# Where attention masks are added to scores: TensorE or VectorE

## The chip, the cores and the metric

The kernel runs on one core of a Trainium2 chip. A core has a matrix engine (TensorE, PE in the profile), which writes its products to PSUM, a memory of eight banks beside the main on-chip memory (SBUF), and engines that work element by element: VectorE (DVE), ScalarE (ACT) and GpSimd (POOL). SyncE (SP) starts the transfers from device memory (DMA). Each engine takes its instructions in order; between engines semaphores say when data are ready. The metric is the time of one execution on the device in microseconds.

## The reference

Two layers of a trunk on 256 tokens of 1024 channels, in fp32. Each layer has a feed-forward part (ffn1), a mixer of four branches, cross-attention to a memory, and a second feed-forward part (ffn2). Two branches of the mixer are attentions, and these are what the change touches:

```python
y_c = nsa_attention(q_n, k_n[:, :, 0], v_n[:, :, 0], k_n[:, :, 1], v_n[:, :, 1],
                    k_n[:, :, 2], v_n[:, :, 2], g_nsa, ...)
...
y_d = banded_attention(q_s, k_s, kv_s[:, :, 1], SWA_WINDOW, swa_sinks[l]).reshape(B, S, BRANCH_W)
gates = jax.nn.sigmoid(u_gate.reshape(B, S, N_BRANCH, D))
branches = (y_a, y_b, y_c, y_d)
merged = gates[:, :, 0] * (y_a @ w_branch[l, 0])
for n in range(1, N_BRANCH):
    merged = merged + gates[:, :, n] * (branches[n] @ w_branch[l, n])
```

and in banded_attention the mask is put on the scores ahead of the softmax:

```python
mask = (diff >= 0) & (diff < window) & (kpos[None, :] >= 0)
s = jnp.einsum('bqgrd,bkgd->bgrqk', qi, ki).astype(jnp.float32) * scale
s = jnp.where(mask, s, NEG_INF)
```

The first attention (NSA, eight heads) has three parts: one over compressed blocks, one over selected blocks, which with 256 tokens are all of them, and one over a window longer than the sequence. The last two need the causal mask alone. The second attention (SWA, eight heads) sees the last 128 tokens.

## The kernel before

Each fp32 weight and each activation is split on the chip into a high part (fp32r, a copy by ScalarE, line 257) and a low part (the difference, by VectorE, line 260), and each product is three matmuls: high by high, high by low, low by high (mm3, lines 273 to 276). The helper matmul on line 271 records nearly all products, so the profile's rows are told apart by their tiles. Weights come in chunks of 2 MB as two halves, raw; ScalarE makes hi and VectorE lo from each.

In the mixer (lines 763 to 920) the tokens lie in two tiles of 128. NSA (nsa) goes through eight units: token tile t, key group g, pair of heads. score makes the scores of a unit in a PSUM bank (acc), and softmax works on them: VectorE's maximum (line 698), ScalarE's exponentials, VectorE's reciprocal. A bank is 128 x 512: for t = 0 it holds two heads by two branches by 128 keys, for t = 1 one head by two branches by 256 keys, so such a unit has two banks. value takes the probabilities (pp) of the unit before: pt_split transposes four blocks of 128 x 128 on PE into a PSUM bank tr (line 722), ScalarE makes pth and VectorE ptl of it, and pv multiplies these with the values (vp). In SWA (swa) one unit is 4 heads for t = 0 and 2 heads for t = 1.

The masks: setup copies two 128 x 128 tiles, "swal" (the window's far edge) and "tri" (causal), 0 or -1e30, to an fp32r tile msk. In score a matmul with the identity idr as the stationary side and the mask as the moving one, repeated over heads by a broadcast view (mtri4, mtri2, mswa), begins the accumulation in the bank, and the products of q with the keys (kkh and kkl in NSA, kks in SWA) are added to it. The profile writes such a product acc<-msk,idr. Per layer there are four of 512 columns and eight of 256 in NSA, and six of 512 in SWA.

Beside the attention VectorE has the taps of a depthwise convolution (conv_taps, 124 per layer, tile cy), whose sums PE takes with a matmul of ones (acc<-cy,ones), the low parts of the weights, and the merge of the branches. PE has products that depend on no attention: the gates (gate_chunk, tiles mm<-hTh,hi and so on), the branches (branch_chunk, mm<-y,hi) and the next projection (tok_major of qs: acc<-hi,hTh). They stand between the attention's steps and fill PE while the other engines work.

The order of all this isn't written out. The tile framework takes the program as written, with priorities for some steps (front, urgent), simulates it with times of its own, and fixes the order of the instructions on each engine by that, with semaphores where data or buffers need them. PSUM is three pools: mm with two buffers, acc with four, tr with two.

Of the kernel before, what the change touches and what calls it, by code (L numbers as in the profile page):

```python
# [8 lines left out]
F32R = mybir.dt.float32r  # L9
# [3 lines left out]
ALU = mybir.AluOpType  # L13
AX = mybir.AxisListType

P = 128
# [11 lines left out]
# ---------------------------------------------------------------- layouts  # L28
# [13 lines left out]
for _n, _w in (("ident", 128), ("tri", 128), ("swal", 128), ("cm", 32), ("vm", 2), ("edge", 64), ("inv", 32), ("ii", 32)):  # L42
    _COFF[_n] = (_NC, _NC + _w)
    _NC += _w
# [159 lines left out]
# ---------------------------------------------------------------- kernel  # L204


class Trunk:
# [28 lines left out]
    # ---- small helpers  # L236
# [55 lines left out]
    # ---- weight stream  # L292
# [24 lines left out]
    def use_spare(self, fn, ahead, at=None):  # L317
        """fn() makes the tiles of the chunk at this distance from the next one to be asked for; it is fetched no
        later than when the chunk at distance at is asked for."""
        self.spare[self.cur + ahead] = fn  # L320
        if at is not None:
            self.early.setdefault(self.cur + at, []).append(self.cur + ahead)
# [26 lines left out]
    # ---- set-up  # L349
# [20 lines left out]
    def setup(self):  # L370
# [12 lines left out]
        msk = self.const.tile([P, 2, P], F32R, name="msk")  # L383
        nc.vector.tensor_copy(msk[:, 0, :], c("swal"))
        nc.vector.tensor_copy(msk[:, 1, :], c("tri"))
# [74 lines left out]
    # ---- norms  # L460
# [9 lines left out]
    def mean_rstd(self, halves, f=1.0):  # L470
        """(f * (mean of squares + eps)) ** -0.5 over two halves of a row."""
# [25 lines left out]
    def boundary(self, gpost, half, gpre, hold=True):  # L497
        """What adds norm(acc) * gpost to a token tile of x, and makes the next norm's transposed halves."""
# [24 lines left out]
    def behind_turn(self, calls, n):  # L523
        """The last n of these calls' matmuls are queued behind the transposes that are pending."""
# [9 lines left out]
    # ---- products  # L534

    def ws(self, out, w, cols, src, nk, k0=0, start=True):
        """out[cols, tok] over nk K-tiles; weights stationary."""
# [4 lines left out]
    def xs_rows(self, nm, nchunks, src, by_tok=2, order=None, by_col=False, then=None):  # L542
        """[tok, 1024] = src^T @ W for chunks of two K-tiles; the last by_tok chunks go token tile by token tile,
        for the second of these in the order given; or column half by column half.  then(t, acc) takes the sums."""
# [40 lines left out]
    # ---- feed-forward  # L585
# [53 lines left out]
    # ---- mixer  # L639
# [10 lines left out]
    def tok_part(self, acc, w, h, n, k0, t, tail=None):  # L650
        """acc[tok, n] += h^T @ W for the K-tiles of one chunk."""
# [36 lines left out]
    def put_v(self, kind, t, ps):  # L688
        """ps: [tok, 2, 64]"""
# [3 lines left out]
    def softmax(self, bank, ng, w, wgt=None, nsink=None, on_dve=False):  # L693
        """bank [P, ng, w] -> normalised (and gated) [P, ng, w] on SBUF."""
# [37 lines left out]
    def pipeline(units):  # L732
        """Each unit is (scores, values): the next unit's scores go before this one's values."""
# [24 lines left out]
    def ypair(self):  # L758
        """hi and lo of four K-tiles."""
# [252 lines left out]
    def blocks(self, ctT, mp):  # L1012
        """Windows of 32 tokens plus their positions, as split [P, 8, hi | lo] tiles."""
# [19 lines left out]
    def compress(self, i, blk, hid):  # L1033
        """Half a product of the compression's first layer; hid gets it, with its bias, after the second half."""
# [51 lines left out]
    def nsa(self, qn, kkh, kkl, gt, y, before_cmp):  # L1086
# [4 lines left out]
        def score(t, g, pr):  # L1091
            h0 = g * 4 + pr * 2
            if t == 0:
                bank = self.pacc((P, 2, 2, P))
                self.matmul(bank.rearrange("p a b k -> p (a b) k"), self.idr, self.mtri4, True, False)
                for j in range(2):
                    q = qn[0][:, h0 + j, :]
                    self.matmul(bank[:, j], q, kkh[:, g, :, 0:P], False, False)
                    self.matmul(bank[:, j], q, kkl[:, g, :, 0:P], False, True)
                wt = self.s(4)  # L1100
# [4 lines left out]
            for j in range(2):  # L1105
                bank = self.pacc((P, 2, S))
                q = qn[1][:, h0 + j, :]
                self.matmul(bank[:, :, P:], self.idr, self.mtri2, True, False)
                self.matmul(bank, q, kkh[:, g], False, False)
                self.matmul(bank, q, kkl[:, g], False, True)  # L1110
                ps.append(self.softmax(bank, 2, S, gt[1][:, h0 + j, 1:3]))
# [65 lines left out]
    def swa(self, qs, kks, y, mp):  # L1177
# [4 lines left out]
        def score(t, g, pr):  # L1182
            if t == 0:
                bank = self.pacc((P, 4, P))
                self.matmul(bank, self.idr, self.mtri4, True, False)
# [168 lines left out]
```

## Time and profile before

| | us |
|---|---|
| median of three runs (1606.2 to 1607.36) | 1607.15 |
| the profiled execution, from first to last instruction | 1605.6 |
| TensorE busy (products) | 1583.0 |
| TensorE busy (weight loads, beside the products) | 1486.1 |
| VectorE busy | 1148.9 |
| ScalarE busy | 860.4 |

The engines work beside each other, so the busy times don't add up to the span. Products on PE are pipelined: one starts before the one ahead of it ends, so a row's duration is longer than the time it takes from PE, and the distance from start to start is the better price. The same holds, less strongly, on VectorE.

### The profile page before, as it was taken

How to read it: one execution, taken by the hardware profiler on the slowest of the kernel's cores; microseconds unless marked ns; L12 is line 12 of the kernel's file. 1: busy time of each engine (PE TensorE's matmuls, PEld its weight loads, DVE VectorE, ACT ScalarE, POOL GpSimd, SP SyncE). 2: the span in 40 equal slices, each digit the busy share in tenths (PEclk: the TensorE clock that was granted, in tenths of full speed). 3: DMA queues.
4: the chain of work that ended last, by engine and by line, in shares of the span. 5: the costliest groups of instructions: out<-in, count | busy, mean ns of one | idle time of the engine just before them, and what ended most of it. 6: DMA issues, size and time to landing. Idle time of an engine off the chain costs nothing.

```text
span 1605.6 us, 28410 instructions
## 1 busy us (share of the span) xinstructions
PE 1583.0 (99%) x11324; PEld 1486.1 (93%) x11324; DVE 1148.9 (72%) x1872; ACT 860.4 (54%) x1461; POOL 21.6 (1%) x44
## 2 busy tenths in 40 slices
PE   7999999999999999999999999999999999999998
PEld 6999889999998989999899988999999999899986
DVE  6665579999878566666566656799998775666653
ACT  6444455665656454444444445656665654554442
POOL 0000000000000000000000000000000000000000
PEclk9999999999999999999999999999999999999999
DMA  7555646643455654555655566465435565455552
GB/s 259 178 181 175 228 154 203 210 132 132 161 170 193 196 176 147 184 184 173 222 172 183 182 198 208 147 222 173 144 120 169 175 211 169 157 169 181 183 195 102
DMA packets 79909, 285.57 MB, mean 178 GB/s; under 512 B 8992, under 2 KB 9760, under 8 KB 79776
## 3 DMA queue, kind: packets, MB, share of 16 engines
q1 hardware_dynamic: 79776, 283.75, 53.5%
q8 instruction: 89, 1.46, 0.3%
q14 instruction: 44, 0.36, 0.1%
HBM read 282.67 MB, written 1.05 MB: 177 GB/s over the span
## 4 chain that ended last, share of the span: by engine, by line
PE 92%; DMA 2%; DVE 2%; ACT 2%; issue 1%; SPq 0%; DVEq 0%; POOLq 0%; ACTq 0%
PE mm L271 54%; PE acc L271 35%; DMA raw<-in_stream_dram 2%; PE tr L465 1%; PE tr L722 1%; ACT hi L257 1%; DVE lo L260 1%; DMA x<-in_x_dram 1%; DVE cy L268 0%; PE tr L271 0%; ACT yw L257 0%; PE tr L684 0%; DVE yw L260 0%; ACT pp L257 0%; PE tr L623 0%
## 5 line engine op out<-in xcount | busy, mean ns | idle before, releaser
L260 DVE TENSOR_TENSOR lo<-raw,hi 128x1024 fp32r<-128x1024 f32 (+1 forms) x468 | 565.8, 1215 | 270.3 <-ACT hi L257 267.4
L257 ACT ACTIVATE hi<-raw 128x1024 fp32r<-128x1024 f32 (+1 forms) x468 | 489.5, 1053 | 359.9 <-PE mm L271 231.4
L271 PE MATMUL mm<-hTh,lo 128*128 128x256 f32 x2048 | 581.6, 284 | 0.0
L271 PE MATMUL mm<-hTh,hi 128*128 128x256 f32 x2048 | 580.9, 284 | 0.4 <-ACT hi L257 0.4
L271 PE MATMUL mm<-hTl,hi 128*128 128x256 f32 x2048 | 580.0, 283 | 0.0
L271 PEld LDWEIGHTS mm<-hTh,hi 128*128 128x128 f32 x2048 | 392.4, 192 | 1.0 <-ACT hi L257 0.8
L271 PEld LDWEIGHTS mm<-hTh,lo 128*128 128x128 f32 x2048 | 392.3, 192 | 0.6
L271 PEld LDWEIGHTS mm<-hTl,hi 128*128 128x128 f32 x2048 | 392.4, 192 | 0.3
L271 PE MATMUL acc<-hi,mid 128*128 128x512 f32 x512 | 159.2, 394 | 0.0
L271 PEld LDWEIGHTS acc<-hi,mid 128*128 128x128 f32 x512 | 96.1, 188 | 23.3
L268 DVE SCALAR_TENSOR_TENSOR cy<-t,sp,cy 128x256 f32<-128x256 f32 x240 | 107.8, 480 | 0.0
L257 ACT ACTIVATE mid<-t 128x256 fp32r<-128x256 f32 x76 | 31.8, 419 | 137.5 <-DVE t L268 137.5
L271 PE MATMUL acc<-lo,mid 128*128 128x512 f32 x256 | 99.7, 397 | 0.0
L271 PE MATMUL mm<-y,hi 128*128 128x256 f32 x512 | 93.7, 282 | 0.0
L271 PE MATMUL acc<-hi,hTh 128*128 128x256 f32 (+2 forms) x272 | 87.8, 324 | 1.7 <-ACT hTh L257 1.6
L271 PE MATMUL acc<-hi,hTl 128*128 128x256 f32 (+2 forms) x272 | 87.8, 323 | 1.3 <-DVE hTl L260 1.3
L271 PE MATMUL acc<-lo,hTh 128*128 128x256 f32 (+2 forms) x272 | 87.6, 322 | 0.0
L271 PEld LDWEIGHTS mm<-y,hi 128*128 128x128 f32 x512 | 79.4, 188 | 1.0
L271 PE MATMUL mm<-y,lo 128*128 128x256 f32 x256 | 72.5, 283 | 0.0
L268 DVE SCALAR_TENSOR_TENSOR t<-t,mm 128x256 f32<-128x256 f32 x160 | 66.8, 418 | 2.6
L257 ACT ACTIVATE t<-acc 128x512 bf16<-128x512 f32 (+3 forms) x56 | 27.2, 487 | 60.4 <-PE acc L271 57.3
L260 DVE TENSOR_TENSOR mid<-t,mid 128x256 fp32r<-128x256 f32 x76 | 32.3, 426 | 36.8 <-ACT mid L257 36.8
(247 smaller groups left out, 2263.1 us busy)
## 6 DMA issues: line engine op xcount, KB each, us to landing
raw<-in_stream_dram SPq DMA_DIRECT2D x508, 512.0 KB, 4.5
g<-in_gains_dram SPq DMA_DIRECT2D x18, 512.0 KB, 4.6
raw<-in_stream_dram SPq DMA_DIRECT2D x8, 280.0 KB, 3.1
t<-in_mem_dram SPq DMA_DIRECT2D x4, 512.0 KB, 4.0
out_dram<-x SPq DMA_DIRECT2D x4, 256.0 KB, 2.0
x<-in_x_dram SPq DMA_DIRECT2D x2, 256.0 KB, 3.1
x<-in_x_dram SPq DMA_DIRECT2D x1, 512.0 KB, 9.0
t<-in_small_dram SPq DMA_DIRECT2D x2, 256.0 KB, 5.6
```

The lines of the kernel that those rows point to most:

```text
L257: return self.nc.scalar.activation(out, in_, func, **kw)
L260: return self.nc.vector.tensor_tensor(out, a, b, op=op)
L268: return self.nc.vector.scalar_tensor_tensor(out, a, s, b, op0=op0, op1=op1)
L271: return self.nc.tensor.matmul(out, lhsT, rhs, start=start, stop=stop, skip_group_check=True)
L465: tr = self.nc.tensor.transpose(pt[:, j, :], xn[:, j * P:(j + 1) * P], self.ident)
L722: self.nc.tensor.transpose(pt[:, j, :], s_, self.ident)
```

## The change

The mask product goes away. The first product of q with a key tile starts the accumulation instead (the start flag), and when the scores are complete, VectorE adds the mask to the bank in place: it reads the bank in PSUM and the mask in SBUF and writes the bank. The softmax then works on the bank as before. 36 matmuls go, 36 additions come: 20 of 128 x 512 and 16 of 128 x 2 x 128, in a bank whose second half of keys alone needs the mask. The two copies into msk go too; the masks are used as fp32 where they were loaded, and for this "swal" and "tri" change places in the table of constants. Comments are left out of the new file, so its later lines have other numbers (722 is 721, 698 is 697, 465 is 464).

```diff
-for _n, _w in (("ident", 128), ("tri", 128), ("swal", 128), ("cm", 32), ("vm", 2), ("edge", 64), ("inv", 32), ("ii", 32)):
+for _n, _w in (("ident", 128), ("swal", 128), ("tri", 128), ("cm", 32), ("vm", 2), ("edge", 64), ("inv", 32), ("ii", 32)):
...
-        msk = self.const.tile([P, 2, P], F32R, name="msk")
-        nc.vector.tensor_copy(msk[:, 0, :], c("swal"))
-        nc.vector.tensor_copy(msk[:, 1, :], c("tri"))
+        a = _COFF["swal"][0] - P
+        msk = cst[:, a:a + 2 * P].rearrange("p (a b) -> p a b", a=2)
...
             if t == 0:
                 bank = self.pacc((P, 2, 2, P))
-                self.matmul(bank.rearrange("p a b k -> p (a b) k"), self.idr, self.mtri4, True, False)
                 for j in range(2):
                     q = qn[0][:, h0 + j, :]
-                    self.matmul(bank[:, j], q, kkh[:, g, :, 0:P], False, False)
+                    self.matmul(bank[:, j], q, kkh[:, g, :, 0:P], j == 0, False)
                     self.matmul(bank[:, j], q, kkl[:, g, :, 0:P], False, True)
+                flat = bank.rearrange("p a b k -> p (a b) k")
+                self.tt(flat, flat, self.mtri4, ALU.add)
                 wt = self.s(4)
                 nc.vector.tensor_copy(wt.rearrange("p (a b) -> p a b", a=2), gt[0][:, h0:h0 + 2, 1:3])
                 p = self.softmax(bank.rearrange("p a b k -> p (a b) k"), 4, P, wt)
...
             for j in range(2):
                 bank = self.pacc((P, 2, S))
                 q = qn[1][:, h0 + j, :]
-                self.matmul(bank[:, :, P:], self.idr, self.mtri2, True, False)
-                self.matmul(bank, q, kkh[:, g], False, False)
+                self.matmul(bank, q, kkh[:, g], True, False)
                 self.matmul(bank, q, kkl[:, g], False, True)
+                self.tt(bank[:, :, P:], bank[:, :, P:], self.mtri2, ALU.add)
                 ps.append(self.softmax(bank, 2, S, gt[1][:, h0 + j, 1:3]))
             return ps
 
...
         def score(t, g, pr):
             if t == 0:
                 bank = self.pacc((P, 4, P))
-                self.matmul(bank, self.idr, self.mtri4, True, False)
                 for r in range(4):
                     q = qs[0][:, g * 4 + r, :]
-                    self.matmul(bank[:, r, :], q, kks[:, g, 0:P], False, False)
+                    self.matmul(bank[:, r, :], q, kks[:, g, 0:P], r == 0, False)
                     self.matmul(bank[:, r, :], q, kks[:, 2 + g, 0:P], False, True)
+                self.tt(bank, bank, self.mtri4, ALU.add)
                 return self.softmax(bank, 4, P, None, ns[:, g * 4:g * 4 + 4], True)
             h0 = g * 4 + pr * 2
             bank = self.pacc((P, 2, S))
-            self.matmul(bank.rearrange("p a (b k) -> p a b k", b=2), self.idr, self.mswa, True, False)
             for j in range(2):
                 q = qs[1][:, h0 + j, :]
-                self.matmul(bank[:, j, :], q, kks[:, g, :], False, False)
+                self.matmul(bank[:, j, :], q, kks[:, g, :], j == 0, False)
                 self.matmul(bank[:, j, :], q, kks[:, 2 + g, :], False, True)
+            quads = bank.rearrange("p a (b k) -> p a b k", b=2)
+            self.tt(quads, quads, self.mswa, ALU.add)
             return self.softmax(bank, 2, S, None, ns[:, h0:h0 + 2], True)
```

The framework's simulation gives other orders on PE, VectorE and ScalarE within the two mixers; the orders of SyncE and GpSimd are the same. Names carry the number of a buffer; a number in the new order is the old one less 3 for the same tile.

PE at the end of NSA in the first layer, from the transposes of probabilities (tr_3704, later tr_3701) on. acc_4608 (later acc_4605) is the next projection, acc_3359 and acc_3569 are NSA's outputs (later 3356 and 3566). Before, from the last of those transposes on:

```order
L722 MATMUL tr_3704<-ident_99,pp_3619 128x128
L271 MATMUL acc_4563<-cy_3803,ones_183 128x256
L271 MATMUL acc_4608<-lo_4611,hTh_2126 128x512
L271 MATMUL acc_4608<-hi_4610,hTl_2127 128x512
L271 MATMUL acc_4608<-hi_4610,hTh_2126 128x512
L271 MATMUL acc_4608<-lo_4611,hTh_2126 128x512
L271 MATMUL acc_4608<-hi_4610,hTl_2127 128x512
L271 MATMUL acc_4608<-hi_4616,hTh_2126 128x512
L271 MATMUL acc_4608<-lo_4617,hTh_2126 128x512
L271 MATMUL acc_4608<-hi_4616,hTl_2127 128x512
L271 MATMUL acc_4608<-hi_4616,hTh_2126 128x512
L271 MATMUL acc_4608<-lo_4617,hTh_2126 128x512
```

The rows that follow it before, up to the first use of ptl_3710, are one more product of the projection (acc_4608<-hi_4616,hTl_2127), four products of pth_3665, pth_3709 and ptl_3666, and four transposes. Now:

```order
L271 MATMUL acc_4605<-hi_4613,hTl_2124 128x512
L271 MATMUL acc_4560<-cy_3800,ones_180 128x256
L271 MATMUL acc_3356<-pth_3662,vc0_196 128x512
L271 MATMUL acc_3566<-pth_3706,vp00_184 128x256
L271 MATMUL acc_3356<-ptl_3663,vc0_196 128x512
L271 MATMUL acc_3356<-pth_3662,vc1_198 128x512
L721 MATMUL tr_3716<-ident_99,pp_3601 128x128
L721 MATMUL tr_3716<-ident_99,pp_3616 128x128
L721 MATMUL tr_3716<-ident_99,pp_3601 128x128
L721 MATMUL tr_3716<-ident_99,pp_3616 128x128
L271 MATMUL acc_4560<-cy_3800,ones_180 128x256
L271 MATMUL acc_3566<-ptl_3707,vp00_184 128x256
```

Ahead of the first of these rows stand the last transposes tr_3701 and one product acc_4605<-lo_4614. From the transposes to the use of ptl stood eleven products of the projection before; two stand there now.

VectorE at the same place. lo is the low part of a weight half, s the softmax's small tiles, pc the compressed part's probabilities, cy the conv's. Before:

```order
L260 TENSOR_TENSOR lo_4611<-raw_4612,hi_4610 128x1024
L268 SCALAR_TENSOR_TENSOR cy_3803<-t4_2774,sp_2236,cy_3803 128x256
L1144 TENSOR_REDUCE s8_3745<-t2_3744 128x8
L260 TENSOR_TENSOR s2_3699<-s2_3699,gt1_2603 128x2
L268 SCALAR_TENSOR_TENSOR cy_3803<-t4_2774,sp_2236,cy_3803 128x256
L260 TENSOR_TENSOR lo_4617<-raw_4618,hi_4616 128x1024
L268 SCALAR_TENSOR_TENSOR cy_3803<-t4_2774,sp_2236,cy_3803 128x256
L260 TENSOR_TENSOR t2_3744<-t2_3744,s8_3745 128x128
L268 SCALAR_TENSOR_TENSOR cy_3803<-t4_2774,sp_2236,cy_3803 128x256
L260 TENSOR_TENSOR ptl_3666<-tr_3660,pth_3665 128x512
L268 SCALAR_TENSOR_TENSOR cy_3803<-t4_2774,sp_2236,cy_3803 128x256
L260 TENSOR_TENSOR ptl_3710<-tr_3704,pth_3709 128x512
```

Now:

```order
L1148 TENSOR_REDUCE s8_3743<-t2_3741 128x8
L268 SCALAR_TENSOR_TENSOR cy_3800<-t4_2771,sp_2233,cy_3800 128x256 x2
L264 TENSOR_SCALAR s8_3743<-s8_3743 128x8
L268 SCALAR_TENSOR_TENSOR cy_3800<-t4_2771,sp_2233,cy_3800 128x256
L1150 RECIPROCAL s8_3744<-s8_3743 128x8
L268 SCALAR_TENSOR_TENSOR cy_3800<-t4_2771,sp_2233,cy_3800 128x256
L260 TENSOR_TENSOR s8_3744<-s8_3744,gt1_2600 128x8
L260 TENSOR_TENSOR ptl_3663<-tr_3657,pth_3662 128x512
L268 SCALAR_TENSOR_TENSOR cy_3800<-t4_2771,sp_2233,cy_3800 128x256
L260 TENSOR_TENSOR pc_201<-t2_3741,s8_3744 128x4x16 x2
L260 TENSOR_TENSOR ptl_3707<-tr_3701,pth_3706 128x512
```

The two low parts of weights (lo_4611, lo_4617) that stood close ahead of ptl_3666 are earlier in the queue now, and conv taps and the compressed softmax's steps stand there. Counted from the start of the queue up to that second ptl, the new order has 12 additions of a mask, ten conv taps and seven short steps of the compressed softmax more than the old one.

PE at the end of SWA in the first layer: acc_5077 (later acc_5074) is its output, mm_5639 are products of a gate, tr_5851 and tr_5860 the transposes of the cross-attention's norm, mm_5699 and mm_5726 the last branch, which takes SWA's output y. Before:

```order
L271 MATMUL acc_5077<-ptl_5169,vp00_187 128x256
L271 MATMUL acc_5077<-pth_5168,vp10_193 128x256
L271 MATMUL acc_5077<-pth_5168,vp01_190 128x256
L271 MATMUL acc_5077<-ptl_5169,vp01_190 128x256
L271 MATMUL acc_5077<-pth_5168,vp11_196 128x256
L271 MATMUL mm_5639<-hTh_2126,hi_5570 128x256
L271 MATMUL mm_5639<-hTl_2127,hi_5570 128x256
L271 MATMUL mm_5639<-hTh_2126,lo_5571 128x256
L271 MATMUL mm_5639<-hTh_2126,hi_5570 128x256
```

32 more products of mm_5639 follow before the branch. Now:

```order
L721 MATMUL tr_5160<-ident_99,pp_5131 128x128 x4
L464 MATMUL tr_5851<-ident_99,t2_5849 128x128 x4
L271 MATMUL acc_5074<-pth_5165,vp00_184 128x256
L271 MATMUL acc_5074<-ptl_5166,vp00_184 128x256
L271 MATMUL acc_5074<-pth_5165,vp10_190 128x256
L271 MATMUL acc_5074<-pth_5165,vp01_187 128x256
L271 MATMUL acc_5074<-ptl_5166,vp01_187 128x256
L271 MATMUL acc_5074<-pth_5165,vp11_193 128x256
L464 MATMUL tr_5860<-ident_99,t2_5858 128x128 x4
L271 MATMUL mm_5699<-y_4952,hi_5624 128x256
L271 MATMUL mm_5726<-y_4952,hi_5624 128x256
```

The gate's products stand ahead of this place now, and the branch follows behind four transposes.

## Rows read from the trace of the kernel before

**Rows 1.** The page: the span, the busy times of the engines, VectorE in 40 equal slices of the span in tenths, and the chain that ended last, by engine.

```profile
span 1605.6 us, 28410 instructions
...
PE 1583.0 (99%) x11324; PEld 1486.1 (93%) x11324; DVE 1148.9 (72%) x1872; ACT 860.4 (54%) x1461; POOL 21.6 (1%) x44
...
DVE  6665579999878566666566656799998775666653
...
PE 92%; DMA 2%; DVE 2%; ACT 2%; issue 1%; SPq 0%; DVEq 0%; POOLq 0%; ACTq 0%
```

**Rows 2.** Busy time of each engine in stretches of 200 us, the two in which the NSA parts of the two mixers lie (columns as the view's head names them: engine, busy us, number of instructions; then the granted clock, the DMA engines' busy share and GB/s).

```profile
200.00:400.00 200.00, 198.74 (x1471) 187.92 (x1470) 183.93 (x386) 121.13 (x244) 1.63 (x3) 1.00 0.51 167
...
1000.00:1200.00 200.00, 198.77 (x1502) 189.57 (x1502) 183.69 (x394) 121.57 (x244) 2.02 (x4) 1.00 0.51 164
```

**Rows 3.** The same view around the first layer's mixer: ahead of NSA, NSA, the turn to the next projection, and the stretch with SWA.

```profile
280.00:289.50 9.50, 9.32 (x72) 8.86 (x71) 9.50 (x20) 4.92 (x8) 0.00 (x0) 1.00 0.80 266
289.50:383.50 94.00, 93.82 (x743) 91.08 (x742) 89.61 (x201) 62.37 (x150) 0.00 (x0) 1.00 0.48 156
383.50:396.00 12.50, 12.22 (x75) 10.47 (x74) 12.22 (x23) 7.94 (x11) 0.00 (x0) 1.00 0.35 119
396.00:470.00 74.00, 74.00 (x621) 73.37 (x620) 60.96 (x114) 44.73 (x95) 1.47 (x3) 1.00 0.47 154
```

**Rows 4.** Groups of instructions by line and shape, the mask products: number, busy us in all, mean ns of one, idle time of the engine just before them.

```profile
L271 PE MATMUL acc<-msk,idr 128*128 128x512 f32 x20 | 7.6, 394 | 0.0
...
L271 PE MATMUL acc<-msk,idr 128*128 128x256 f32 x16 | 4.5, 280 | 0.0
```

**Rows 5.** PE's timeline around the first mask product (start, duration, instruction).

```profile
289.47 0.39 PE L271 MATMUL acc<-msk,idr 128*128 128x512 f32 x1
289.70 0.28 PE L271 MATMUL acc<-kkh,q 128*128 128x256 f32 x1
289.81 0.28 PE L271 MATMUL acc<-kkl,q 128*128 128x256 f32 x1
```

**Rows 6.** VectorE's groups in NSA's stretch: those that read PSUM (tr and acc lie there).

```profile
L260 DVE TENSOR_TENSOR ptl<-tr,pth 128x512 fp32r<-128x512 f32 x10 | 6.8, 682 | 1.9 <-ACT pth L257 1.9
...
L268 DVE SCALAR_TENSOR_TENSOR y<-acc,sp,y 128x256 fp32r<-128x256 f32 x2 | 0.9, 482 | 0.0
L1143 DVE TENSOR_REDUCE t<-acc 128x128 f32<-128x256 f32 x2 | 0.8, 412 | 0.0
```

**Rows 7.** VectorE's timeline where a subtraction from PSUM stands in a full queue.

```profile
311.89 0.48 DVE L268 SCALAR_TENSOR_TENSOR cy<-t,sp,cy 128x256 f32<-128x256 f32 x1
312.28 0.68 DVE L260 TENSOR_TENSOR ptl<-tr,pth 128x512 fp32r<-128x512 f32 x1
312.88 0.87 DVE L268 SCALAR_TENSOR_TENSOR cy<-t,sp,cy 128x256 f32<-128x256 f32 x2
```

**Rows 8.** What PE waited for over the whole program: us in all, times, longest.

```profile
PE tr L465 <- DVE t L268: 10.2, 1, 10.2
PE acc L271 <- ACT hTh L257: 1.6, 1, 1.6
...
PE acc L271 <- DVE ptl L260: 0.5, 2, 0.2
```

**Rows 9.** The end of NSA in the first layer: rows of PE's timeline and then one of VectorE's.

```profile
375.11 0.58 PE L271 MATMUL acc<-hi,hTh 128*128 128x512 f32 x1
375.53 0.39 PE L271 MATMUL acc<-lo,hTh 128*128 128x512 f32 x1
...
378.72 0.60 PE L722 MATMUL tr<-ident,pp 128*128 128x128 f32 x4
...
379.40 0.59 PE L271 MATMUL acc<-lo,hTh 128*128 128x512 f32 x1
379.83 0.40 PE L271 MATMUL acc<-hi,hTl 128*128 128x512 f32 x1
...
383.30 0.36 PE L271 MATMUL acc<-ptl,vp 128*128 128x256 f32 x1
...
380.55 0.68 DVE L260 TENSOR_TENSOR ptl<-tr,pth 128x512 fp32r<-128x512 f32 x1
```

**Rows 10.** The last pieces of NSA: PE, then ScalarE and VectorE.

```profile
391.40 0.60 PE L722 MATMUL tr<-ident,pp 128*128 128x128 f32 x4
391.84 0.60 PE L271 MATMUL acc<-cy,ones 128*128 128x256 f32 x2
...
392.95 0.47 PE L271 MATMUL acc<-pth,vp 128*128 128x256 f32 x1
393.65 0.38 PE L271 MATMUL acc<-ptl,vp 128*128 128x256 f32 x1 [0.23 <-DVE ptl L260]
...
392.04 0.60 ACT L257 ACTIVATE pth<-tr 128x512 fp32r<-128x512 f32 x1 [0.66 <-PE tr L722]
...
392.91 0.69 DVE L260 TENSOR_TENSOR ptl<-tr,pth 128x512 fp32r<-128x512 f32 x1
```

**Rows 11.** From an attention's last product to its split output: PE, ScalarE, VectorE.

```profile
382.71 0.39 PE L271 MATMUL acc<-pth,vc 128*128 128x512 f32 x1
...
383.14 0.60 ACT L257 ACTIVATE y<-acc 128x512 fp32r<-128x512 f32 x1 [2.94 <-PE acc L271]
...
383.77 0.69 DVE L260 TENSOR_TENSOR y<-acc,y 128x512 fp32r<-128x512 f32 x1 [0.48 <-ACT y L257]
```

## The prediction

> **What bounds the kernel now.** I read the page from the top. TensorE (PE) is busy 1583.0 of 1605.6 us, VectorE (DVE) 1148.9 us or 72%, and the chain that ended last is 92% PE [rows 1]. The list of PE's waits says the same: apart from 10.2 us at the start no wait of PE is longer than 1.6 us [rows 8]. So over the whole program an instruction taken off PE should shorten it by what PE spent on it, and one given to DVE should be free.
>
> The masks, though, stand in the two mixers alone, and there the average doesn't hold. In 200 to 400 us and 1000 to 1200 us DVE is busy 183.93 and 183.69 of 200 us [rows 2], and while the first attention (NSA) runs, 289.5 to 383.5 us, it is busy 89.61 of 94.00 us: it has 4.4 us of idle time in all, at a granted clock of 1.00 [rows 3]. That is where most of the new work goes. In the second attention (SWA), 396 to 470 us, it has 13 us to spare [rows 3].
>
> **What goes from PE.** 20 mask products of 512 columns and 16 of 256 [rows 4]. Their listed 394 and 280 ns overlap with their neighbours and aren't what PE pays: a mask product starts at 289.47, the next product at 289.70, a 256-column one at 289.81 [rows 5]. So 0.23 and 0.12 us each: 20 x 0.23 + 16 x 0.12 = 6.5 us; NSA's share is 4 x 0.23 + 8 x 0.12 = 1.9 us per layer. Nothing hides it, PE having no gaps there. The two casts that made the mask tile at set-up stood ahead of PE's first work or beside it; I count nothing for them.
>
> **What DVE gets.** 36 additions, read from PSUM and written back there. No row shows DVE writing PSUM. The nearest is the subtraction that reads PSUM and writes SBUF, 682 ns for 512 columns [rows 6], of which the next instruction sees 0.60 us (312.28 to 312.88) [rows 7]. For 256 columns the reads of PSUM list 412 ns (a reduction) and 482 ns (two operations) [rows 6]; with the same 0.09 us overlapped, 0.33 to 0.39. I take 0.60 and 0.33: NSA 4 x 0.60 + 8 x 0.33 = 5.0 us, SWA 6 x 0.60 = 3.6 us per layer, 17.3 in all. A conv tap, which touches SBUF alone, has a pitch of 0.39 for 256 columns (311.89 to 312.28) [rows 7], so 0.33 isn't a high price. Bounds: above, no overlap at all, 0.69 and 0.48 (NSA 6.6), and twice my price as the far end, should writing PSUM be slow (NSA 10); below, half of it (NSA 2.5), as no row rules out that an addition in place is quicker.
>
> The Trainium skill, "VectorE: DVE Perf Modes", section "The DRAIN you can't avoid", says that the next DVE operation does not start before the pipe is empty. By that rule an addition would cost its whole 0.69 us, and NSA's additions some 1 us more per layer. The row decides against it here: the follower starts 0.09 us before the listed end [rows 7].
>
> **Where DVE's time lands on PE.** Orders are static, so I compared them. The place is the end of NSA: a transposed piece of the probabilities (tr) is split by ScalarE (pth) and DVE (ptl), and PE then multiplies with it. Up to the second ptl of the pair shown (ptl_3710, now ptl_3707) DVE's queue now holds 12 additions (5.0 us), ten more conv taps at 0.39 (3.9 us) and a handful of short softmax pieces that moved ahead (0.9 us): 9.9 us more. PE arrives 1.9 us sooner, since twelve mask products ahead of it are gone. In the trace that ptl starts at 380.55 and ends 0.68 later, at 381.23, and PE's first product with it starts at 383.30: 2.07 us of slack [rows 9]. The idle time of 4.4 us that DVE had in NSA is filled first. What is left is 9.9 + 1.9 - 2.07 - 4.4 = 5.3 us that PE stands still, per layer.
>
> Before, PE had something to do meanwhile: between the transposes and that use stood eleven products of the next projection (acc_4608, 0.23 us each); now two stand there, because the scheduler used the fill earlier. So the wait isn't covered. It takes the place of small stalls of today: 375.11 to 375.53 and 379.40 to 379.83 are each 0.2 us over a product's 0.23, and 392.95 to 393.65 is 0.58 over 0.12 [rows 9, 10]. That is 1.0 us per layer which I count as gone. Net 4.3 us per layer.
>
> At the end of SWA the queue is short, but the fill is gone as well. The order had 36 gate products (mm_5639) between the last product of the attention and the first of the last branch; now the gates are used up before. From the end of four transposes' issue (391.40 to 391.84) through pth (392.04 to 392.64) and ptl's 0.69 us [rows 10] it takes 1.5 us until PE can go on; in the new order a set of four transposes (0.44) and one product (0.12) lie between: 0.9 us of stall. Then the last product, its two evacuations and the branch: in the trace 382.71 to the end of y's second half, 384.46 [rows 11], 1.75 us, against 0.8 us of work in between (the product itself, four transposes, two products): 0.95. Together 1.8 us per layer, which today isn't there.
>
> **The sum**, against the profiled execution's span of 1605.6 us: -6.5 + 2 x 4.3 + 2 x 1.8 = +5.7 us, so 1611.3 us of span. The median of the runs is 1607.15 us, 1.55 us above that span; the same offset gives 1612.9, and I forecast 1613 us.
>
> The bounds of the terms: if DVE's idle time outside NSA (16.1 us from 200 to 400, of which 4.4 lie in NSA [rows 2, 3]) also takes 2 us of the lateness, by work drawn ahead, and SWA's two chains are half covered, the stalls are 2 x (5.3 - 2 - 1) + 2 x 0.9 = 6.4 us, and the net is zero. If the additions cost 0.69 and 0.48, NSA's stall grows by 1.6 us per layer, and if none of the 1.0 us goes away by another 1.0, the net is 5.7 + 5.2 = +11 us, 1618. Twice the price would add 2 x 5.0 to the sum: +16, 1623. Half of it makes the two stalls 2.5 us shorter each: about +1, 1608.
>
> **Rivals.**
>
> *The average is right.* PE is the engine that everything waits for, and DVE's queue takes the additions without making PE wait. For it: PE 99%, DVE 72% [rows 1], and of all its waits PE owes ptl no more than 0.5 us today [rows 8]. It needs DVE's lateness never to reach a ptl; then only chains of latency remain, about 1 us per layer at either attention's end, against the 1.0 us that goes. Time: 1607.15 - 6.5 + 2 to 3, about 1603, at best 1600.7. Against it: rows 3. The Trainium skill's "Perfetto Trace Analysis", section "Identifying the Most-Contended Engine", speaks for this rival (optimise the engine with the highest occupancy first); its section "Optimization Strategy" allows that this engine changes from regime to regime, and rows 3 show such a stretch.
>
> *It comes out even.* The stall at NSA's end is about half of mine, because DVE can put conv taps off or its earlier idle time absorbs the start. Stalls equal the 6.5 us saved: 1604 to 1610.
>
> *The addition is dear.* PSUM to PSUM costs DVE well over the subtraction's 0.60 us. In NSA every 0.1 us more per addition makes 12 x 0.1 = 1.2 us per layer, 2.4 in all, once the queue is late; it ends slower than today wherever the price is above about half of what I took. 1618 to 1623. Nothing in the trace speaks for or against it but that the reading side has the usual price.
>
> *That the masks aren't applied by DVE at all* I don't see: the order has 36 additions and no product with msk.
>
> **Chances.** What a measurement of this kernel can tell from no change is 0.2%, 3.2 us. My case (1610 to 1617): 0.48. Dear additions (above 1617): 0.11. Even (1604 to 1610): 0.22. The average (under 1604): 0.19. Leaving out about 0.1 on either side, the range is 1602 to 1620; my own case alone would be 1609 to 1617. Slower by over 0.2% (above 1610.4): 0.57; within 0.2%: 0.23; faster (under 1603.9): 0.20.
>
> **What would show it.** In the profile of the changed kernel: 36 DVE rows acc<-acc,cst, at about 690 and 420 ns, and DVE's sum up by 17 us or a little more; no msk row on PE. In NSA's stretch DVE busy over 99% of it. In the list of PE's waits, ptl of DVE with several us in place of 0.5 us, and at SWA's end waits for ptl and for y of around a us each. PE's own busy time would fall by some us in spite of the longer span. I am wrong if DVE keeps idle time in NSA while PE waits less than 2 us per layer for ptl (then the queue isn't what matters), or if PE waits there for the weight subtractions lo, which would put the lateness elsewhere, or if the additions' rows are far from 690 ns.

## The result: 1626 us, slower by 1.2%

The changed kernel takes 1626.33 us (median of four, 1625.46 to 1629.23) against 1607.26 us: the ratio is 1.0123, with an interval of 1.0111 to 1.0135. The forecast had the direction, but not the size: 1613 us with a range to 1620.

The page of the changed kernel first: the span, the engines' busy times, and VectorE's slices.

```profile
span 1627.4 us, 28371 instructions
...
PE 1591.6 (98%) x11288; PEld 1489.4 (92%) x11288; DVE 1165.6 (72%) x1906; ACT 860.5 (53%) x1461; POOL 21.6 (1%) x44
...
DVE  6665579999778576665566656799988785666653
```

Against [rows 1] PE has 36 instructions fewer and is nevertheless busy 8.6 us longer. An engine that does less and takes longer ran slower, or its pipelined products lay further apart. Both happened, in stretches such as these (the view of [rows 2 and 3]: PE, weight loads, VectorE, ScalarE, POOL, then the granted clock):

```profile
200.00:400.00 200.00, 195.41 (x1417) 183.43 (x1416) 184.62 (x392) 120.53 (x243) 1.63 (x3) 0.98 0.49 160
...
289.50:345.00 55.50, 55.09 (x454) 54.05 (x453) 55.50 (x118) 35.69 (x86) 0.00 (x0) 1.00 0.57 185
345.00:369.50 24.50, 24.50 (x203) 24.17 (x201) 22.58 (x50) 15.78 (x36) 0.00 (x0) 1.00 0.40 131
369.50:383.50 14.00, 10.64 (x43) 8.28 (x42) 14.00 (x43) 9.73 (x27) 0.00 (x0) 0.76 0.23 76
476.00:490.00 14.00, 10.90 (x75) 10.03 (x74) 7.63 (x14) 5.69 (x11) 1.09 (x2) 0.88 0.56 187
```

VectorE is busy every moment from 289.5 to 345 us, PE is idle for 0.4 us of that, and then, from 369.5 to 383.5 us, PE issues 43 products in 14 us at a mean clock of 0.76. The end of SWA (476 to 490) shows the same in small. The clock fell in five stretches of the program and in none of the kernel before but its last 3 us; inside them the rows are:

```profile
375.80:382.50 6.70, 6.15 (x22) 5.40 (x23) 6.70 (x26) 3.96 (x13) 0.00 (x0) 0.50 0.02 6
409.90:413.20 3.30, 3.30 (x18) 3.30 (x17) 0.36 (x2) 0.00 (x0) 0.03 (x1) 0.50 0.18 72
485.00:488.30 3.30, 3.08 (x15) 3.02 (x15) 1.55 (x3) 0.00 (x0) 0.00 (x0) 0.50 0.41 154
1133.60:1136.90 3.30, 3.30 (x17) 3.20 (x16) 3.30 (x6) 0.00 (x0) 0.00 (x0) 0.50 0.11 32
1184.80:1191.50 6.70, 6.12 (x23) 5.25 (x24) 6.70 (x26) 4.14 (x13) 0.00 (x0) 0.50 0.11 43
```

The granted clock is 0.50 there, which is the level of 1.2 GHz. PE's waits, to be compared with [rows 8]:

```profile
PE tr L464 <- DVE t L268: 9.7, 1, 9.7
PE acc L271 <- DVE ptl L260: 3.8, 5, 1.2
PE acc L271 <- ACT pp L257: 3.8, 6, 1.3
...
PE mm L271 <- ACT y L257: 1.6, 2, 1.4
PE acc L271 <- ACT pth L257: 1.4, 2, 0.9
PE tr L721 <- ACT pp L257: 1.3, 2, 1.0
```

How the 19 us come about can be added up from the starts of PE's products. For each product I took how much later its follower started than is usual for its kind (the median over the program of products with the same tiles and shape), and summed. Before: 17.5 us in the whole program. Changed: 33.4 us where the clock was 1.00, and 11.5 us more inside the five slow stretches. So some +16 us of waiting, +12 us at the half clock, and -6.5 us of products that are gone: +21, where the spans differ by 21.8 us and the medians by 19.1. Another way of telling kinds apart moves each of the two by about a microsecond. (The profiled execution of the changed kernel, at 1629.23 us, is the longest of its four.)

One place in detail, PE at the end of NSA in the first layer:

```profile
369.47 0.40 PE L271 MATMUL acc<-kkl,q 128*128 128x512 f32 x1
370.87 0.55 PE L721 MATMUL tr<-ident,pp 128*128 128x128 f32 x3 [1.01 <-ACT pp L257]
371.75 0.55 PE L721 MATMUL tr<-ident,pp 128*128 128x128 f32 x3 [0.33 <-ACT pp L257]
372.66 0.50 PE L271 MATMUL acc<-kkh,q 128*128 128x512 f32 x1 [0.36 <-ACT pp L257]
...
373.23 0.31 PE L271 MATMUL acc<-pth,vp 128*128 128x256 f32 x1
374.11 0.39 PE L271 MATMUL acc<-ptl,vp 128*128 128x256 f32 x1 [0.56 <-DVE ptl L260]
...
375.63 0.49 PE L271 MATMUL acc<-ptl,vp 128*128 128x256 f32 x1 [0.54 <-DVE ptl L260]
375.93 0.63 PE L271 MATMUL acc<-pth,vp 128*128 128x256 f32 x2
376.35 0.41 PE L271 MATMUL acc<-ptl,vp 128*128 128x256 f32 x1
376.57 0.41 PE L271 MATMUL acc<-pth,vp 128*128 128x256 f32 x1
376.78 0.41 PE L271 MATMUL acc<-cmneg,idr 128*128 128x256 f32 x1
```

Between 369.5 and 375.6 us PE waits five times, for the probabilities (pp) and then for their low part (ptl). At 375.8 the clock falls: two products of 256 columns that stood 0.11 us apart in [rows 5] now start 0.21 us apart (375.93, two of them, to 376.35). Not every one of the five falls stands behind such waits. Ahead of the one at 409.9 us PE had waited only 0.3 us since 383 us, and had worked off 16 products of a single column (405.8 to 407.8 us); the same 16 are in the kernel before (from 398.1 us) and in the second layer of the changed one (from 1211.4 us), with no fall behind them.

Why are the probabilities late? VectorE in the unit ahead, from one addition to the maximum of the same bank (the bank whose addition is at 358.92 has its maximum at 363.17, by the order in which these stand; the addition at 362.83 is of the next bank):

```profile
358.92 0.43 DVE L260 TENSOR_TENSOR acc<-acc,cst 128x256 f32<-128x256 f32 x1
359.26 0.69 DVE L260 TENSOR_TENSOR ptl<-tr,pth 128x512 fp32r<-128x512 f32 x1
359.85 0.48 DVE L268 SCALAR_TENSOR_TENSOR cy<-t,sp,cy 128x256 f32<-128x256 f32 x1
...
360.52 0.88 DVE L268 SCALAR_TENSOR_TENSOR cy<-t,sp,cy 128x256 f32<-128x256 f32 x2
361.30 1.23 DVE L260 TENSOR_TENSOR lo<-raw,hi 128x1024 fp32r<-128x1024 f32 x1
362.44 0.49 DVE L268 SCALAR_TENSOR_TENSOR cy<-t,sp,cy 128x256 f32<-128x256 f32 x1
362.83 0.44 DVE L260 TENSOR_TENSOR acc<-acc,cst 128x256 f32<-128x256 f32 x1
363.17 0.69 DVE L697 TENSOR_REDUCE s<-acc 128x2 f32<-128x512 f32 x1
```

The addition takes 0.34 us (358.92 to 359.26). The maximum that needs it starts 4.25 us after it, because the queue holds a ptl, conv taps and a weight's low part in between. The chain from scores to exponentials used to stand in VectorE's queue once and now does so twice. I call each such step of a chain, which has to wait until the queue reaches it, a turn. From the start of a bank's last score product to its first exponential, mean over NSA's 24 banks: 6.2 us before, 10.7 us now; SWA 5.2 and 6.9. From addition to maximum, mean of all 36: 5.1 us.

ScalarE's queue adds to it. The probabilities that PE waits for at 370.87 were scaled at 370.33, though VectorE had had the factor ready at 365.5 us:

```profile
363.02 0.90 ACT L257 ACTIVATE pp<-pp,s 128x256 f32<-128x256 f32 x2
...
367.87 1.06 ACT L257 ACTIVATE hi<-raw 128x1024 fp32r<-128x1024 f32 x1 [2.84 <-PE mm L271]
369.36 1.06 ACT L257 ACTIVATE hi<-raw 128x1024 fp32r<-128x1024 f32 x1 [0.43 <-PE mm L271]
370.33 0.49 ACT L257 ACTIVATE pp<-pp,s 128x256 f32<-128x256 f32 x1
```

Two splits of weights stand ahead of it in the order, and these wait for PE to give their buffers back. No trial takes this part out by itself.

The additions themselves cost what was forecast (listed duration; the follower of a 512-column one starts 0.60 us after it):

```profile
L260 DVE TENSOR_TENSOR acc<-acc,cst 128x512 f32<-128x512 f32 x20 | 13.8, 700 | 2.0 <-PE acc L271 2.0
...
L260 DVE TENSOR_TENSOR acc<-acc,cst 128x256 f32<-128x256 f32 x16 | 6.9, 433 | 1.2 <-PE acc L271 1.2
```

### The profile page after: what moved, and what is told of

It reads as the page before. It is cut to its first block, busy times and chain, and to the rows that moved or that the text cites. A ratio compares the mean times of both kernels' runs of the same rounds, so it can differ in the third digit from the quotient of the medians.

```text
span 1627.4 us, 28371 instructions
## 1 busy us (share of the span) xinstructions
PE 1591.6 (98%) x11288; PEld 1489.4 (92%) x11288; DVE 1165.6 (72%) x1906; ACT 860.5 (53%) x1461; POOL 21.6 (1%) x44
## 5 line engine op out<-in xcount | busy, mean ns | idle before, releaser
L271 PE MATMUL mm<-y,hi 128*128 128x256 f32 x512 | 97.5, 289 | 2.4 <-ACT y L257 1.6
L271 PEld LDWEIGHTS acc<-lo,mid 128*128 128x128 f32 x256 | 48.1, 188 | 12.1 <-DVE lo L260 1.0
```

The lines of the kernel that those rows point to most:

```text
L271: return self.nc.tensor.matmul(out, lhsT, rhs, start=start, stop=stop, skip_group_check=True)
```

## The experiments

Three questions: is it the additions or the new order of the instructions; if the additions, is it VectorE's time or their place in the chain; and can the loss be taken out. All times are medians; the kernel before, run beside them, was between 1606.9 and 1607.3 us. Every trial gets an order of instructions of its own from the framework's simulation, so a difference between two trials is that of the edit together with its order.

**Which half, and whether it is the additions.** The first and the second trial have the change in one attention alone, the third leaves the masks out in the changed kernel.

```diff
# e1_nsa_only: score of nsa as in the change, score of swa as before; e2_swa_only the other way round
# e3_neither
-                self.tt(flat, flat, self.mtri4, ALU.add)
...
-                self.tt(bank[:, :, P:], bank[:, :, P:], self.mtri2, ALU.add)
...
-                self.tt(bank, bank, self.mtri4, ALU.add)
...
-            self.tt(quads, quads, self.mswa, ALU.add)
```

> Masks by VectorE in NSA, by matmuls as before in SWA. If the parts add, NSA alone carries the stalls at its end and the drops of the clock behind them, which the trace of the change shows as 8.7 us of stalls and 11.4 us at the half clock, less 3.7 us of mask products: 1607 + 16.4 = about 1623 us. If the loss is spread by the order as a whole (the scheduler's fill), no such sum holds, and it may be anywhere from 1605 to 1626.

> Masks by VectorE in SWA, by matmuls as before in NSA. If the parts add: 4.7 us of stalls and 1.9 us at the half clock, less 2.8 us of mask products: about 1611 us. If SWA's stall is only there because NSA used the fill up before it, there is none here: 1607 - 2.8 = 1604 us.

> Leaves the causal and local masks out: no mask products and no additions. If VectorE's additions cause the stalls (its full queue, or their place in the chain of the softmax), they go, and with them the drops of the clock: 1607 - 6.5 = 1600.7 us. If what hurts is that the products' removal lets the scheduler use the fill sooner, stalls remain: 1607 to 1620 us.

Measured: 1618.74 us (ratio 1.0073, 1.0058 to 1.0088), 1615.96 us (1.006, 1.0043 to 1.0077) and 1602.47 us (0.9973, 0.9964 to 0.9983). With neither, PE's waits for the probabilities are down to 0.7 us in all and the slow stretches are gone, so it is the additions and not the products' removal; the time is 1.8 us above the 1600.7 expected. The two halves add up to 20.8 us, near the whole, but NSA alone costs 4 us less than expected and SWA alone, 9 us, twice what I read from the trace of the change: it has its stall also when NSA leaves the fill alone (two waits of 0.5 and 1.0 us and one of 2.0 us before the last branch), and a clock of 0.50 from 476.5 to 483.4 us. There, with SWA alone changed, VectorE's queue is not full:

```profile
466.00:484.00 18.00, 14.54 (x95) 13.64 (x95) 9.39 (x16) 7.10 (x16) 1.08 (x2) 0.81 0.52 173
```

VectorE is busy 9.39 of 18 us. What has grown is the chain: from the last score product to the first exponential it takes SWA 7.4 us in this trial, against 5.2 before.

**The additions beside the products.**

```diff
                 self.matmul(bank.rearrange("p a b k -> p (a b) k"), self.idr, self.mtri4, True, False)
...
+                self.tt(flat, flat, self.ftri4, ALU.add)
```

(and so at the three other places)

> The mask products stay and VectorE adds the masks on top of them, in the same places as the change does: PE is not relieved, VectorE and the chain of the softmax are loaded as in the change. If the additions alone make the loss, it is 25 us without the 6.5 us of gain: 1625 to 1634 us. If the loss needs the products' removal as well (less work for PE to fill the waits with), clearly less: 1612 to 1622 us.

Measured: 1631.32 us (1.015, 1.0135 to 1.0165). The additions alone make the loss, 24 us of it.

**Less work for VectorE.** First the last three taps of each channel group left out, then 23 of 31, with a control on the kernel before:

```diff
-        for j in range(31):
+        for j in range(28):      # e5_fewer_taps; range(8) in e7_after_8taps and e7b_before_8taps
```

> The change, with the last three of 31 taps of the convolution left out: 12 operations of 0.39 us, 4.7 us less on VectorE per layer, which is what NSA's additions put on it. If VectorE's full queue in NSA is the cause, NSA's stalls and clock drops go and SWA's remain: about 1607 - 6.5 + 6.6 = 1607 us or less, 1600 to 1609. If it is the longer chain from scores to probabilities, or the fill used up early, it stays slow: 1618 to 1627 us.

> The change, with 23 of the 31 taps of the convolution left out, 92 operations or 36 us less on VectorE per layer, so that its queue is no longer full in NSA whatever the order. If the full queue is the cause, NSA's stalls and clock drops go and SWA's remain: 1607 us or less. If the longer chain is the cause, NSA's end stays slow: 1615 us or more.

> The kernel before with 23 of the 31 taps left out, as control for the change with 8 taps (1604.2 us). If the short queue makes the change harmless, it is within 4 us of that; if leaving taps out quickens the program by itself, it is 1590 us or less, and the change still costs its 19 us.

Measured: 1626.35 us (1.012, 1.0105 to 1.0135), 1604.18 us (0.9983, 0.9974 to 0.9993) and 1605.39 us (0.9988, 0.9979 to 0.9998). The first was a badly chosen edit: the three taps come last, the scheduler fills VectorE with the others, and 289.5 to 345 us is as full as it was (55.50 of 55.50 us), with PE waiting at the same place. It decides nothing. With 8 taps the queue is short, as NSA's stretch shows (the change, then the control):

```profile
289.50:383.50 94.00, 92.59 (x742) 90.90 (x741) 68.21 (x139) 63.79 (x154) 0.00 (x0) 0.98 0.44 143
```

```profile
289.50:383.50 94.00, 94.00 (x765) 92.34 (x764) 64.41 (x129) 65.78 (x156) 0.00 (x0) 1.00 0.45 146
```

From addition to maximum it is 2.7 us now on the mean, and the change loses nothing on balance: 1604.2 against 1605.4 us. It isn't free either, since of the 6.5 us of PE's products 1.2 us are gained; one wait of 1.4 us for the gates is left (until 298.9 us), with a clock of 0.50 from 300.4 to 303.8 us. So the loss needs VectorE's long queue. This doesn't yet tell time from place, since a short queue also makes a second turn cheap.

**Time without place.** About the same amount of VectorE's work on a scratch tile, masks by products:

```diff
+        self.zz = self.const.tile([P, 2, P], BF16, name="zz")
...
+                self.tt(self.zz, self.offm, self.offm, ALU.add)
```

> The masks stay products on PE; beside them VectorE does as many additions as in the change, at the same places of the program, 256 columns at a time (52 of them, about 17 us), but on a scratch tile that nothing waits for. If VectorE's queue being full is the cause, it is as slow as the kernel with both: 1615 us or more. If it is the addition's place in the chain from scores to probabilities, the scratch work costs nothing or little: 1606 to 1611 us.

Measured: 1609.6 us (1.0012, 1.0003 to 1.0022). It looks like an answer and is none. There were 56 pieces rather than 52, and the scheduler, finding nothing that they depend on, put all of them at the start of the program:

```profile
L260 DVE TENSOR_TENSOR zz<-ident x56: 416/422/430, 8.2 to 74.5; 128x256 bf16<-128x256 f32 x56
```

The last columns are the first and last start. So it was tried again, each piece pinned behind the instruction traced before it on VectorE, the maximum of its bank or the first piece (the trace shows them from 292.3 to 1262.5 us, in the two mixers):

```diff
         nc.vector.tensor_reduce(nm, bank, axis=AX.X, op=ALU.max, negate=True)
+        for _ in range(off):
+            self.tc.keep_in_program_order(self.tt(self.zz, self.offm, self.offm, ALU.add))
```

> The first trial with scratch additions put all of them at the program's start (the trace shows them from 8 to 75 us), so it said nothing of NSA. Here each is queued behind the maximum of its bank: 56 additions of 256 columns, 24 us of VectorE, inside NSA and SWA, which nothing waits for; masks by products as before. If VectorE's time in the full queue is what hurts, 1615 us or more. If only work inside the softmax's chain does, 1606 to 1611 us.

Measured: 1620.63 us (1.0084, 1.007 to 1.0097). Nothing waits for this work, and yet it costs 13 us. PE's waits say by which way:

```profile
PE acc L271 <- DVE cy L268: 4.9, 2, 4.5
PE acc L271 <- DVE s L260: 3.3, 1, 3.3
```

In both the product that waits is one of the conv's taps (acc<-cy,ones), which are the end of VectorE's queue in NSA: 4.5 us from 375.2 us and 3.3 us in the second layer, and in the first the clock falls meanwhile (0.50 from 376.4 to 383.3 us). So VectorE's time does matter in NSA. It took 23.1 us of scratch work to do this, more than the additions' 20.7 us.

**Place without time.** The additions cut to 16 columns:

```diff
-                self.tt(flat, flat, self.mtri4, ALU.add)
+                self.tt(flat[:, 0:1, 112:], flat[:, 0:1, 112:], self.mtri4[:, 0:1, 112:], ALU.add)
```

(and so at the three other places)

> The change with the additions cut to 16 columns of each bank (the rest of the masks is left out): 36 additions at the same places of the softmax's chain, but some 0.1 us each instead of 0.60 and 0.33. If it is the additional turn in VectorE's queue that makes the loss, most of it stays: 1615 us or more. If it is the time that the additions take on VectorE, it goes: about the 1602.5 us of the kernel with no mask, up to 1607.

Measured: 1612.49 us (1.0032, 1.0021 to 1.0043), between the two expectations.

```profile
L260 DVE TENSOR_TENSOR acc<-acc,cst 128x16 f32<-128x16 f32 x36 | 6.1, 174 | 2.8 <-PE acc L271 2.8
```

36 instructions of 0.17 us stand 4.4 us on the mean ahead of their maximum and cost 10 us against the kernel with no mask (1602.5). So the additional turn, with 6.1 us of VectorE's time in it, makes some 10 of the 24 us, and what the full-sized additions bring beyond it 14; both shares hold for these two orders.

**Covering the waits for ptl.** The products of pth go ahead of those of ptl:

```diff
+        for i, (n, vh, vl) in enumerate(parts):
+            self.matmul(out, vh, p[0][:, n, :], start and i == 0, False)
+            self.matmul(out, vl, p[0][:, n, :], False, False)
+        for i, (n, vh, vl) in enumerate(parts):
+            self.matmul(out, vh, p[1][:, n, :], False, stop and i == len(parts) - 1)
```

> The change, with the products of the high parts of the probabilities (pth) ahead of those of the low parts (ptl) in each step of the values: four products instead of one stand between ScalarE's part and VectorE's, 0.36 us more cover at each wait for ptl. The trace of the change has five such waits of 0.7 to 1.3 us beside those for pp and y. If stalls are what matters, about 2 us of them go, and if the clock drops hang on the length of the stalls, some of the 12 us they cost with them: 1612 to 1624 us. If neither, 1626 us.

Measured: 1626.18 us (1.0117, 1.0102 to 1.0132), no gain. The waits for ptl are down from 3.8 to 0.5 us, and those for the probabilities have grown in their place, from 3.8 to 8.1 us:

```profile
PE acc L271 <- ACT pp L257: 8.1, 8, 1.9
PE tr L721 <- ACT pp L257: 2.2, 2, 1.1
PE acc L271 <- ACT pth L257: 1.8, 3, 1.3
```

What PE waits for last is not what makes the chain late; the wait moved up the chain.

**One turn instead of two.** First by an instruction that adds and takes the extreme:

```diff
-        nc.vector.tensor_reduce(nm, bank, axis=AX.X, op=ALU.max, negate=True)
...
+                nc.vector.tensor_tensor_reduce(v, v, m, -1.0, 1e38, ALU.add, ALU.min, nm[:, i:i + 1])
```

> VectorE adds the mask and takes the row maximum in one instruction per head and branch (the sum is written back negated with its minimum beside it, and ScalarE's exponential takes the sign back), so that a bank's scores wait for VectorE's queue once, as before the change, instead of twice; no mask products. VectorE's work is about that of the change (sum of addition and reduction, in 96 pieces instead of 72). If the second turn in the queue is what lengthens the chain, the stalls go: 1601 to 1606 us. If VectorE's time is what hurts, nothing is gained: 1618 us or more.

Measured: 1630.86 us (1.0148, 1.0133 to 1.0164). Such an instruction yields one number per row, so a bank takes four or two of them, and each took its own turn: in NSA's first four units 11.9 us pass on the mean from the start of a bank's first piece to that of its last. SWA's stall is nearly gone (1.1 us), NSA's is worse. Expected and edit were at odds: this made more turns, not fewer. Then without the maximum, in the change and in the kernel before:

```diff
-        nc.vector.tensor_reduce(nm, bank, axis=AX.X, op=ALU.max, negate=True)
...
-            self.act(p[:, i, :], bank[:, i, :], AF.Exp, bias=nm[:, i:i + 1], accum_out=l[:, i:i + 1])
+            kw = {} if nomax else {"bias": nm[:, i:i + 1]}
+            self.act(p[:, i, :], bank[:, i, :], AF.Exp, accum_out=l[:, i:i + 1], **kw)
```

> The change without the maximum in NSA's and SWA's softmax (exponentials of the scores as they are, which with these inputs are small enough; SWA's sinks likewise): the addition is the only turn in VectorE's queue between scores and exponentials, as the maximum was before the change, and VectorE's work is less than before. If the turn is what counts, all of the loss goes and the gain of 6.5 us is there: 1599 to 1603 us, faster than both kernels. If an addition in place in PSUM has a cost of its own, it stays slow: 1615 us or more.

> The kernel before, masks by products, also without the maximum: no turn in VectorE's queue between scores and exponentials. If the chain of the softmax is hidden in the kernel before, taking a turn out of it brings nothing: 1604 to 1608 us, the small stalls at NSA's end at most. If it bounds it already, 1600 us or less.

Measured: 1600.83 us (0.9961, 0.9948 to 0.9973) and 1606.76 us (1.0, 0.9991 to 1.0009). With the addition as the only turn, 6.2 of the 6.5 us of the products are gained, and the changed kernel is the fastest of all. NSA in it, and its additions:

```profile
289.50:383.50 94.00, 94.00 (x740) 90.94 (x739) 89.62 (x211) 60.54 (x152) 0.00 (x0) 1.00 0.46 154
```

```profile
L260 DVE TENSOR_TENSOR acc<-acc,cst 128x512 f32<-128x512 f32 x20 | 13.3, 690 | 0.0
L260 DVE TENSOR_TENSOR acc<-acc,cst 128x256 f32<-128x256 f32 x16 | 6.7, 420 | 0.0
```

VectorE's NSA stretch is as full as before the change (89.62 against 89.61 us), PE is busy in all 94 us, and the clock stays at 1.00 but for the program's last microsecond or so. So the maximum's time has gone with its turn, and this pair doesn't tell the two apart; it shows that the additions in PSUM cost next to nothing once the maximum makes room for them. Taking the maximum out of the kernel before brings nothing, since its chain was hidden already. The price is that these exponentials are no longer guarded against large scores.

## Why the prediction fell short

**What bounds it**: right for NSA, where VectorE's full queue was the place, and the program's average of 72% (still 72%) said nothing. That reading is what decided against the rival of the average; with one step fewer (no maximum) that rival's outcome does come about, and with a short queue (8 taps, 1604.2 us) nearly. For SWA it is half the story: with VectorE busy only about half of the time around the stall, the change in SWA alone costs 9 us.

**What goes from PE, 6.5 us**: right. The kernel without the maximum gains 6.2 us of it, the one with no mask 4.5 us.

**What an addition costs**: right. 700 and 433 ns listed, and 0.33 to 0.34 us from start to start for 256 columns (362.83 to 363.17). The dear addition was no part of it; the time of 1626 us lies beyond that rival's range for another reason.

**Where it lands**: right in the attention, wrong in the spot and in the way. I had priced the addition as 5.0 us of backlog ahead of one late ptl, ptl_3707. At that one PE loses 0.18 us. It stands earlier, at the pair before it (369.5 to 376 us), since the chain has one turn more in a full queue, some 4 to 5 us per bank, in which the fill is used up. Backlog (the pinned scratch work, 13 us) and turn (16 columns, 10 us) each turned out to cost. By its own sign of being wrong the prediction fails here: VectorE keeps 1.9 us of idle time in NSA (345 to 369.5 us), so is busy 98% of it and not over 99%, and PE waits for ptl less than 2 us there, and longer for pp. The queue matters all the same, one step further up the chain.

**The stalls' size**: right within a few microseconds, though partly by luck, given the wrong spot. By the starts of PE's products (after less before, at a clock of 1.00), NSA waits 3.4 us more in the first layer and 6.4 in the second, where I had 4.3 each; SWA 4.2 and 0.9, where I had 1.8 each. Together 14.9 us against 12.2. About 1 us more lies elsewhere in the program.

**The term that failed** is one that the sum did not have: "-6.5 + 2 x 4.3 + 2 x 1.8 = +5.7 us" priced a wait at its own length and put the clock at nothing. In the changed kernel the clock fell to 0.50 five times, for 3.4 or 6.8 us, four of them right behind PE's waits in the attentions, and the products in there took about twice as long: some 12 us lost in the five stretches (half of 3 x 3.4 and 2 x 6.8 us), nearly as much as the waits in the attention. For the same reason the sign that PE's busy time would fall by some us didn't come: it rose by 8.6 us. The rows I had read showed a clock of 1.00 wherever I looked, and I took it as given. In the kernels with few waits in the mixers (no mask; no maximum, either way) the clock does not fall before the end. That the waits bring it down is argued from this; a run that holds PE busy through the waits, to separate the two, was not made.

**The range** ended at 1620 us because its dearest case for the waits, +11 us, had no clock in it. With the 12 us its upper end would have been 1632.

## What to carry to other kernels

Price an instruction that moves to another engine not only by its time but by the turn that it adds: in an in-order queue that is full at that place, a dependent step of 0.17 us stood 4.4 us ahead of the next one, and NSA's chain from scores to exponentials took 9.6 us with it, against 6.8 in the kernel with no mask. The Trainium skill, "VectorE: DVE Perf Modes", section "Rules for kernel authors", asks VectorE's users to minimise the number of operations, there because of the pipeline flush behind each one. That reason no run here shows, but 36 short operations cost 10 us, more than the 6.1 us for which they keep VectorE busy. And where a change may make PE wait for some microseconds in a row, add the clock to the sum, for it can double the price of the wait; look first for a turn to take out in exchange (here the maximum, whose time goes too).

## What was not expected of the hardware

That the clock falls behind waits of a few microseconds, in a kernel whose PE is busy for 98% of its span, I had not expected; the longest stretches at 0.50 took 10.2 us (with NSA alone changed, 374.6 to 384.8 us, for one). It did not follow every cluster of waits: in the trial with three taps fewer, SWA's end had 3.0 us of waiting between 474 and 480.2 us with no fall behind it, while 1.9 us in the changed kernel before 1133.1 us were followed by one, and so was the single wait of 1.4 us with 8 taps. What decides between these the runs do not show.
